# A mixture-of-experts decoder block on one core: smaller token blocks for some experts, and the last four blocks' sums kept on chip

## The chip, the cores and the metric

The kernel runs on one core of a Trainium2 chip. Its time is device time in microseconds (us) for one execution of the whole block; three timed runs of the kernel before gave a median of 1283.62 us (1282.87 to 1284.56). Beside them one execution was recorded by the hardware profiler. Times in the traces count from the start of that execution's span. TensorE is called PE and its weight loads PEld, VectorE DVE, ScalarE ACT, GpSimd POOL and SyncE SP.

## The reference

One decoder layer for 1024 tokens of width 1024, all in float32: a conditioned norm, attention and a gated branch, then a mixture of 32 experts in 4 groups of 8, and a final RMS norm. A token picks one group and two experts in it. Cut to what the change touches:

```python
g_idx = argmax(lg); top_p, top_i = top_k(softmax(le of that group), 2)
expert_id = g_idx * 8 + top_i                       # two experts of one group per token
yb = (silu(xb @ w_gate[e]) * (xb @ w_up[e])) @ w_down[e]   # 1024 -> 512 -> 1024, blocks of rows xb of expert e
x = x + g2 * segment_sum(yb * row_weight, token)
y = x * rsqrt(mean(x * x) + eps) * final_g          # final norm
```

Which tokens an expert gets is known only at run time. With these inputs the 32 experts get between 8 and 226 of the 2048 token places.

## The kernel before, in words

The first stage, up to about 682 us, ends with the router. This document is about the second stage, from there to the end: 32 units, one per expert. The first four units are expert 0 of each group, fixed when the kernel is built, so that their weights and rows can be fetched before the routing is sorted. The other 28 are taken from a list that the kernel sorts at run time: groups by their largest expert, and experts within a group by their count. `PLAN` gives the rows that a place in that list may hold, `TURNS` the order in which the places are taken. A unit whose count exceeds its rows would go through a loop at the very end, which with these inputs is not entered.

A unit needs gate, up and down weights, 2 MiB each. They come through `ring2`, a ring of seven 2 MiB buffers of the pool `big`: SP issues load k (line 1343) when the buffer of load k-7 has been read. The order is gate of unit u, down of unit u-1, up of unit u. The work itself is a list of jobs (`jobs2`), four to a load. Functions hooked onto a job are put into the program behind it: the gather of rows by POOL (`gather`, line 1364), the transposes on PE (`x_t`, `a_t`), `silu` and `mul`, and `y_out`, which scales the result on DVE (lines 1506, 1510) and adds its rows to the residual array `x1d` in DRAM by an indirect DMA on POOL (line 1493).

Blocks come in two sizes. In a **128-row block** each weight piece of 128x1024 is split into a high and a low part, by a cast on ACT (line 443) and a subtraction on DVE (line 444), two jobs ahead of its use; the parts lie in the pool `h2p` with four buffers each; PE makes three passes (`mm3`, lines 132 to 134). In a **64-row block** the raw weights are read by PE directly (`PSH`, line 1432): two instructions, one for each half of the 128 columns of the array, so that the two halves of the output columns are computed side by side. So the buffers of a 128-row block come free when DVE has split them, those of a 64-row block when PE has read them.

While the first units run, `table` (hooked on jobs 7 to 14) makes the row lists of all other blocks from one-hot products on DVE, POOL and PE, once for whole blocks and once for halves.

At the end `f_load` (line 1725), hooked onto the down jobs of the third last unit but queued on SP behind all loads of the ring, issues eight loads of 512 KiB that bring `x1d` back, and then the last unit's down weights in four parts. The results of the last two blocks (`ends`, both of 64 rows) are not added in DRAM: their rows of `x1d` are gathered, added and normed apart. `final` (lines 1781 to 1817) squares the eight token tiles on ACT (line 1736), scales them on DVE (line 1746), and stores everything by POOL's indirect DMAs (line 1764): the tiles without the rows of the last two blocks (`rows_o` sends those out of bounds), and these rows by themselves.

## Time and profile before

| | |
|---|---|
| timed runs | 1283.62 us median of 3 (1282.87 to 1284.56) |
| the profiled execution's own time | 1281.95 us |
| its span | 1280.3 us |
| expert stage | about 682 us to the end of the span |
| TensorE busy | 1189.3 us, 93% of the span |
| VectorE, ScalarE, GpSimd busy | 820.0, 595.2 and 236.3 us |
| moved by DMA | 334.25 MB, mean 261 GB/s over the span |

The share of a whole span hides that the first stage is limited by arithmetic and moves little, while the second moves 192 MiB of expert weights. So the second is read by stretches: for each the busy time of the engines, the share of the DMA engines, and who waited for whom. A DMA share of 1 means that all sixteen engines had packets all the time; the rows about SP's queue tell which buffer a load waited for before it could even be issued.

### The profile page before, as it was taken

The page shows a single profiled execution, that of the slowest core. Times are in us where ns is not written, and L with a number is a line of the kernel's source. Part 1 is how long each engine was busy: PE and PEld are TensorE (multiplying, and loading weights), DVE is VectorE, ACT ScalarE, POOL GpSimd, SP SyncE. Part 2 cuts the span into 40 slices and gives each one's busy share as a digit, 9 for nine tenths or more (in the row PEclk, how much of TensorE's full clock was granted, in tenths as well). Part 3 has the DMA queues.
Part 4 walks back from the last instruction along what each step waited for, and adds up shares of the span by engine and source line. Part 5 has one row for each costly group of instructions (what it writes and reads, how often), then busy time and mean ns, then how long its engine had stood idle before and what let it go on. Part 6 is the DMA issues. An engine that isn't in the chain of part 4 may idle for free. (4 is left out here: it accounts for less than half of the span.)

```text
span 1280.3 us, 17327 instructions
## 1 busy us (share of the span) xinstructions
PE 1189.3 (93%) x6243; PEld 911.5 (71%) x6244; DVE 820.0 (64%) x1699; ACT 595.2 (46%) x1005; POOL 236.3 (18%) x262
## 2 busy tenths in 40 slices
PE   6999999999989999899997999999999999899881
PEld 3788887788879888688875786676665655776540
DVE  7668885568667888344598896675434612984406
ACT  4459743236535774233345585563314512773321
POOL 3510010011140001010233322212112121111114
PEclk8899999999989999899996999999999999999996
DMA  9634446566443435534766699999999999999975
GB/s 321 216 108 124 132 135 203 174 212 230 131 169 118 127 127 183 179 99 147 288 245 233 215 366 405 400 406 399 376 333 405 383 336 407 409 411 390 412 274 218
DMA packets 106885, 334.25 MB, mean 261 GB/s; under 512 B 8883, under 2 KB 52611, under 8 KB 82344
## 3 DMA queue, kind: packets, MB, share of 16 engines
q1 hardware_dynamic: 91286, 292.46, 60.3%
q0 software_dynamic: 15408, 40.59, 10.7%
q8 instruction: 50, 0.82, 0.3%
q14 instruction: 43, 0.35, 0.1%
q10 hardware_dynamic: 98, 0.03, 0.0%
HBM read 315.98 MB, written 27.54 MB: 268 GB/s over the span
## 5 line engine op out<-in xcount | busy, mean ns | idle before, releaser
L444 DVE TENSOR_TENSOR lo<-big,hi 128x1024 fp32r<-128x1024 f32 x192 | 227.7, 1223 | 44.8 <-ACT hi L443 44.3
L132 PE MATMUL ps<-big,hi 128*128 128x512 f32 x544 | 220.3, 405 | 7.8 <-ACT hi L443 7.8
L443 ACT CAST hi<-big 128x1024 fp32r<-128x1024 f32 x192 | 196.4, 1050 | 60.9 <-PE ps L134 58.3
L133 PE MATMUL ps<-big,hi 128*128 128x512 f32 x544 | 217.1, 399 | 3.3 <-DVE big L444 3.3
L134 PE MATMUL ps<-big,lo 128*128 128x512 f32 x544 | 216.3, 398 | 0.0
L443 ACT CAST hi<-st 128x512 fp32r<-128x512 f32 x192 | 116.1, 619 | 204.2 <-PE ps L133 120.1
L444 DVE TENSOR_TENSOR lo<-st,hi 128x512 fp32r<-128x512 f32 x192 | 135.5, 717 | 105.5 <-ACT hi L443 104.8
L1432 PE MATMUL ps<-big,xTh 128*64 128x256 f32 x1088 | 128.8, 383 | 0.0
L132 PEld LDWEIGHTS ps<-big,hi 128*128 128x128 f32 x544 | 105.3, 193 | 31.4 <-ACT hi L443 9.3
L133 PEld LDWEIGHTS ps<-big,hi 128*128 128x128 f32 x544 | 105.2, 193 | 29.4 <-DVE big L444 4.8
L134 PEld LDWEIGHTS ps<-big,lo 128*128 128x128 f32 x544 | 104.8, 193 | 23.1 <-DVE lo L444 1.1
L133 PE MATMUL ps<-lo,xTh 128*128 128x512 f32 x272 | 110.5, 406 | 8.4 <-DVE lo L444 8.3
L132 PE MATMUL ps<-hi,xTh 128*128 128x512 f32 x272 | 112.2, 414 | 6.2 <-ACT hi L443 6.2
L134 PE MATMUL ps<-hi,xTl 128*128 128x512 f32 x272 | 108.8, 400 | 0.3 <-DVE xTl L444 0.3
L1432 PEld LDWEIGHTS ps<-big,xTh 128*64 128x64 f32 x1088 | 74.5, 137 | 43.1 <-issue 4.6
L132 PE MATMUL ps<-hi,big 128*128 128x256 f32 (+1 forms) x256 | 88.4, 346 | 0.0
L133 PE MATMUL ps<-lo,big 128*128 128x256 f32 (+1 forms) x256 | 86.8, 339 | 0.7 <-DVE lo L444 0.7
L134 PE MATMUL ps<-hi,big 128*128 128x256 f32 (+1 forms) x256 | 86.5, 338 | 0.0
L1432 PE MATMUL ps<-big,aTh 128*64 128x512 f32 x272 | 64.7, 614 | 8.7 <-DMA big<-in_w_down_dram 8.7
L133 PEld LDWEIGHTS ps<-lo,xTh 128*128 128x128 f32 x272 | 52.0, 191 | 23.2 <-DVE lo L444 12.9
L132 PEld LDWEIGHTS ps<-hi,xTh 128*128 128x128 f32 x272 | 51.8, 191 | 23.3 <-ACT hi L443 9.2
L1469 DVE TENSOR_TENSOR sl<-sl,ps 128x512 f32<-128x512 f32 (+1 forms) x34 | 18.8, 552 | 70.0 <-PE ps L1432 48.1
(365 smaller groups left out, 1942.6 us busy)
## 6 DMA issues: line engine op xcount, KB each, us to landing
big<-in_w_gate_dram SPq DMA_DIRECT2D x32, 2048.0 KB
big<-in_w_up_dram SPq DMA_DIRECT2D x32, 2048.0 KB
big<-in_w_down_dram SPq DMA_DIRECT2D x30, 2048.0 KB
st<-in_w_in_dram SPq DMA_DIRECT2D x26, 1024.0 KB
st<-in_w_ada_dram SPq DMA_DIRECT2D x16, 1024.0 KB
st<-in_w_o_dram SPq DMA_DIRECT2D x10, 1024.0 KB
big<-in_x_dram SPq DMA_DIRECT2D x16, 512.0 KB
bias<-biasd POOLq DMA_DIRECT2D x16, 512.0 KB, 4.6
```

The source lines that it names most:

```text
L132: PE.matmul(ps, lh, rh, start=start, stop=False)
L133: PE.matmul(ps, lh, rl, start=False, stop=False)
L134: PE.matmul(ps, ll, rh, start=False, stop=stop)
L443: ACT.copy(hi, src)
L444: return DVE.tensor_tensor(lo, src, f(hi), op=OP.subtract)
L1432: PE.matmul(ps[64 * c:64 * c + 64], xt[:, j, 64 * h:64 * h + 64], w[:, n * c:n * c + n], start=start, stop=stop)
L1469: DVE.tensor_tensor(s, s, PS.pop((i, "u"))[:, 0:s.shape[1]], op=OP.mult)
```

## The change

In short: three of the four first experts, which were 128-row blocks, become 64-row blocks (`FIRST`, `FIRST_ROWS`: one group's first expert, that of group 1, stays whole and goes first). In `PLAN` the 13 whole blocks stay, of its 17 halves six become 32-row blocks, for which `side` uses four column groups of 32 columns. So the stage has 14 whole, 14 half and 6 quarter blocks where it had 17 whole and 17 half. The array `x1d` is called `zd`. `TURNS` of one group is changed so that the last four blocks have 64, 32, 32 and 32 rows; these four are now `ends`: their rows of `zd` are gathered in the second last unit (`z_get`), and their results stay on chip. The last four units thus add nothing to `zd`, and `f_load` is hooked onto the down jobs of the second last unit; its place in SP's queue stays. The output is now stored in two steps: the eight tiles whole, by SP's queue, and then the rows of the last four blocks over them, by POOL. Tables are made once, for 128 rows, and the lists for halves and quarters are folded from them (`rows_table`); `visits` takes the second part of a split expert into account. `tab_tok` makes six products per tile where it made two. `h2p` has three buffers, not four.

```diff
+        ((128, 64), (128,), (128,), (64,), (64,), (32,), (32,)),
+        ((128,), (128,), (64,), (64,), (64,), (64,), (32,)),
+        ((128,), (128,), (64,), (64,), (32,), (32,), (32,)))
+FIRST = (1, 0, 2, 3)
+FIRST_ROWS = (128, 64, 64, 64)
-TURNS = ((5, 1, 0, 2, 6, 3, 4), (1, 3, 4, 0, 5, 2, 6), (2, 0, 3, 4, 1, 5, 6), (0, 2, 3, 4, 1, 5, 6))
+TURNS = ((5, 1, 0, 2, 4, 3, 6), (1, 3, 4, 0, 5, 2, 6), (2, 0, 3, 4, 1, 5, 6), (0, 2, 3, 4, 1, 5, 6))
...
         for k in range(2):
-            PE.matmul(ps, A[:, k], C[:, k], start=(t == 0 and k == 0), stop=(t == 7 and k == 1))
+            at = dict(start=(t == 0 and k == 0), stop=(t == 7 and k == 1))
+            PE.matmul(ps[0:64, 0:4], A[:, k, 0:64], V[:, k, 0], **at)
+            PE.matmul(ps[64:128, 0:4], A[:, k, 64:128], V[:, k, 1], start=at["start"], stop=False)
+            PE.matmul(ps[64:128, 0:4], A[:, k, 0:64], V[:, k, 2], start=False, stop=at["stop"])
...
-    ends = flat[-2:]
+    ends = flat[-4:]
...
+    def z_get(i):
+        with tc.issue_after(R["gather"].ins), tc.issue_after(adds[-1][1].ins):
+            g_ = fetch(Z[i], zd, IDX[i][1], parts(i))
...
-    def PSH(ps, xt, h, j, w, n, start, stop):
-
-        for c in range(2):
-            PE.matmul(ps[64 * c:64 * c + 64], xt[:, j, 64 * h:64 * h + 64], w[:, n * c:n * c + n], start=start, stop=stop)
+    def side(c, ps, xt, i, w, inner, start, stop):
+
+        n, q = rows_of[c], parts(c)
+        m = w.shape[1] // q
+        for e in range(q):
+            cols_w = w[:, m * e:m * e + m]
+            if inner and q == 4:
+
+                cols_w = w.rearrange("k (h p j) -> k h j p", h=2, j=2)[:, e // 2, e % 2]
+            PE.matmul(ps[n * e:n * e + n, 0:m], xt[:, n * i:n * i + n], cols_w, start=start, stop=stop)
...
-            if u < NE - 1:
-                jobs2.hook(jd, lambda pv=pv: each(y_out, pv))
-            if u == NE - 2:
-                jobs2.hook(jd, lambda: f_load())
+            jobs2.hook(jd, lambda pv=pv: each(y_out, pv))
...
+        if u == NE - 2:
+            jobs2.hook(jg[1], lambda: each(z_get, ends))
+    f_at = jd
...
-    h2p = p2.enter_context(tc.tile_pool(name="p2hl", bufs=4, reuse_waits="tile"))
+    h2p = p2.enter_context(tc.tile_pool(name="p2hl", bufs=3, reuse_waits="tile"))
...
+    def f_put(t):
+        xt = F["x"][t // 4][:, t % 4]
+        DVE.scalar_tensor_tensor(xt, xt, fs[:, t:t + 1], FG, op0=OP.mult, op1=OP.mult)
+        SP.dma_start(out[t * P:t * P + P, :], xt)
+
+    def l_sq(j):
+        z, y = (t[ends[j]][:, 0:D // parts(ends[j])] for t in (Z, YL))
+        DVE.tensor_tensor(z, z, y, op=OP.add)
+        ACT.activation(y, z, AF.Square, accum_out=fs[:, 8 + j:9 + j])
...
+            mul(ends[3])
+            a_t(ends[3])
+            for j in range(3):
+                l_sq(j)
+            for t in range(4):
+                f_sq(t)
+            rsqrt(wk, fs[:, 0:4], 4, 1.0 / D)
+            for t in range(4):
+                f_sq(4 + t)
+                f_put(t)
+            rsqrt(wk, fs[:, 4:8], 4, 1.0 / D)
+            l_norm(0, 3)
+            for k in range(4):
+                d_mm(ends[3:], k, F["w"])
+            f_put(4)
+            f_put(5)
+            y_out(ends[3])
+            l_sq(3)
+            f_put(6)
+            f_put(7)
+            l_norm(3, 4)
+            for j in range(4):
+                l_put(j)
+    jobs2.hook(f_at, f_load)
```

`l_norm` folds the sums of squares of a split row by products on PE, takes the root, and scales each column part by itself; `l_put` stores one of the four blocks' rows.

TensorE at the head of the stage, where the first units meet. Before, behind the down projection of the first unit (`xg` are gathered rows that are transposed, `hi` and `lo` the parts of split weights, `tV` a table):

```order
L1392 MATMUL ps_7731<-ident,xg_7449 128x128 x4
L1392 MATMUL ps_7738<-ident,xg_7449 128x128
L1678 MATMUL ps_7508<-tV_7693,tA_7689 128x68 x2
L1687 MATMUL ps_7509<-tV_7693,tA_7702 128x68 x2
L1392 MATMUL ps_7738<-ident,xg_7449 128x128 x3
L132 MATMUL ps_7753<-hi_7679,xTh_7433 128x512
L133 MATMUL ps_7753<-lo_7680,xTh_7433 128x512
L134 MATMUL ps_7753<-hi_7679,xTl_7434 128x512
```

The same place now (`big` are raw weights, `ps_7787` the second unit's up projection, `ps_7816` the third unit's gate):

```order
L1790 MATMUL ps_7748<-y_7737,fold 128x68
L1439 MATMUL ps_7775<-ident,xg_7557 128x128 x4
L1495 MATMUL ps_7787<-big_7017,xTh_7550 64x256 x16
L1495 MATMUL ps_7816<-big_7419,xTh_7774 64x256 x4
L1543 MATMUL ps_7821<-ident,sl_7679 128x128 x2
L1495 MATMUL ps_7816<-big_7419,xTh_7774 64x256 x12
L1495 MATMUL ps_7842<-big_7421,aTh_7824 64x512 x8
```

The three-pass products of the second to fourth unit are gone, and with them their splits on ACT and DVE; one table product per tile is left, and two fold products follow the last one.

GpSimd at the end of the program. Before (`y` are results added to the residual array, `big` its eight tiles, `xg` the rows of the last two blocks):

```order
L1493 DMA x1d<-y_11686,tok_h 2048x512
L1364 DMA xg_11792<-x1d,late_i 128x512
L1364 DMA xg_11796<-x1d,late_i 128x512
L1764 DMA out_dram<-big_11691,rows_o 1024x1024 x4
L1764 DMA out_dram<-big_11692,rows_o 1024x1024 x3
L1764 DMA out_dram<-xg_11792,tok_h 2048x512
L1764 DMA out_dram<-xg_11796,tok_h 2048x512
L1764 DMA out_dram<-big_11692,rows_o 1024x1024
```

And now, from the last add on (`z` are the gathered rows of the last four blocks, `big_11833` their results):

```order
L1412 DMA zd<-y_11456,rows_i 4096x256
L1407 DMA z_7406<-zd,rows_i 128x512
L1407 DMA z_7409<-zd,rows_i 128x256
L1407 DMA z_7412<-zd,rows_i 128x256
L1407 DMA z_7415<-zd,rows_i 128x256
L1412 DMA out_dram<-big_11833,rows_i 2048x512
L1412 DMA out_dram<-big_11833,rows_i 4096x256 x3
```

The stores of the eight tiles have left GpSimd for SyncE's queue; four stores are left, all behind the last tile.

VectorE at the end. Before, from the fifth tile on:

```order
L1746 SCALAR_TENSOR_TENSOR big_11692<-big_11692,fs,hi_11599 128x1024 x2
L1506 SCALAR_TENSOR_TENSOR y_11882<-ps_11863,w_h,g2h 128x512
L1792 TENSOR_TENSOR xg_11796<-xg_11796,y_11882 128x512
L1746 SCALAR_TENSOR_TENSOR big_11692<-big_11692,fs,hi_11599 128x1024
L1742 COPY fs<-ps_11891 128x2
```

And now (behind three roots, the last of them that of the first three of the four blocks):

```order
L1869 SCALAR_TENSOR_TENSOR big_11833<-z_7406,fs,fgr 64x512 x2
L1869 SCALAR_TENSOR_TENSOR big_11833<-z_7409,fs,fgr 32x256 x4
L1869 SCALAR_TENSOR_TENSOR big_11833<-z_7412,fs,fgr 32x256 x4
L1847 SCALAR_TENSOR_TENSOR big_11786<-big_11786,fs,fgr 128x1024 x2
L1569 SCALAR_TENSOR_TENSOR y_7416<-ps_11929,w_sb,g2r 32x256 x4
L1852 TENSOR_TENSOR z_7415<-z_7415,y_7416 128x256
L1847 SCALAR_TENSOR_TENSOR big_11786<-big_11786,fs,fgr 128x1024 x2
L1863 COPY fs<-ps_11960 128x1
```

A block of 32 rows takes four small products where one stood, and ten of them, two of 64 rows and eight of 32, lie between the tiles' products.

## Rows read from the trace of the kernel before

**Rows 1.** The view by stretches of time over the whole expert stage. Columns: stretch in us from the span's start, its length, busy us of PE, PEld, DVE, ACT and POOL (instructions in brackets), the granted clock of TensorE (1 is full speed), the busy share of the sixteen DMA engines, GB/s.

```profile
680.00:740.00 60.00, 52.18 (x249) 41.54 (x250) 52.76 (x119) 34.89 (x41) 19.96 (x25) 0.89 0.63 222
740.00:910.00 170.00, 165.10 (x876) 120.79 (x875) 118.47 (x131) 93.92 (x112) 38.72 (x21) 1.00 1.01 394
910.00:940.00 30.00, 30.00 (x151) 21.25 (x150) 12.59 (x13) 10.99 (x14) 3.37 (x2) 1.00 0.89 343
940.00:1020.00 80.00, 77.80 (x453) 49.91 (x451) 34.84 (x38) 28.34 (x37) 16.78 (x12) 1.00 1.01 390
1020.00:1040.00 20.00, 20.00 (x122) 11.12 (x122) 8.36 (x10) 5.26 (x8) 3.40 (x3) 1.00 0.81 290
1040.00:1220.00 180.00, 170.14 (x960) 115.33 (x958) 96.16 (x103) 78.08 (x99) 30.58 (x22) 0.99 1.02 403
1220.00:1240.00 20.00, 20.00 (x134) 10.00 (x132) 1.17 (x2) 2.90 (x6) 2.79 (x3) 1.00 0.56 194
1240.00:1252.00 12.00, 3.28 (x28) 1.89 (x24) 3.40 (x16) 8.03 (x16) 2.11 (x2) 0.77 1.02 404
1252.00:1281.00 29.00, 6.34 (x18) 2.12 (x18) 17.16 (x42) 2.00 (x6) 12.94 (x10) 0.62 0.48 189
```

**Rows 2.** What SyncE's DMA queue waited for between 740 and 1240 us: line, releaser, us in total, times, longest.

```profile
SPq L1343 <- DVE lo L444: 218.9, 40, 9.6
SPq L1343 <- PE ps L1432: 198.1, 41, 14.0
SPq L1728 <- DMA x1d<-y,tok_h: 24.7, 1, 24.7
```

**Rows 3.** The same view of TensorE, same stretch.

```profile
PE ps L132 <- ACT hi L443: 9.0, 6, 2.1
PE ps L133 <- DVE lo L444: 7.5, 11, 1.1
```

**Rows 4.** The timeline of SyncE's queue: start us, us, line, the transfer issued, count; two pieces of it, at the head and at the end of the stage. A ring load moves 2 MiB.

```profile
733.50 0.39 SPq L1343 DMA_DIRECT2D big<-in_w_gate_dram  x1
...
743.93 0.38 SPq L1343 DMA_DIRECT2D big<-in_w_up_dram  x1
...
1212.53 0.37 SPq L1343 DMA_DIRECT2D big<-in_w_up_dram  x1
1237.72 4.01 SPq L1728 DMA_DIRECT2D big<-x1d  x8
1241.97 4.23 SPq L1348 DMA_DIRECT2D big<-in_w_down_dram  x4
```

**Rows 5.** The timeline of TensorE, columns as in rows 4, with the tile shape of the array (128\*64: two column groups of 64) and the operand's shape. First a load's worth of a 64-row gate or up projection, then the first and the last of 21 consecutive matmuls of a 128-row block, then the period of one 64-row unit after another and its down projection.

```profile
970.35 3.67 PE L1432 MATMUL ps<-big,xTh 128*64 128x256 f32 x32
...
976.25 0.40 PE L132 MATMUL ps<-hi,xTh 128*128 128x512 f32 x1
...
980.92 0.40 PE L134 MATMUL ps<-hi,xTl 128*128 128x512 f32 x1
...
1048.67 4.54 PE L1432 MATMUL ps<-big,xTh 128*64 128x256 f32 x40
...
1056.22 3.60 PE L1432 MATMUL ps<-big,aTh 128*64 128x512 f32 x16
...
1060.43 1.95 PE L1432 MATMUL ps<-big,xTh 128*64 128x256 f32 x16
```

**Rows 6.** Groups of instructions between 740 and 1240 us by line and shape: count, busy us, mean ns, idle time before them and its releasers. The weight load of a 64-row block, the two steps of a 128-row block's weight split, and a 256-column product on VectorE.

```profile
L1432 PEld LDWEIGHTS ps<-big,xTh 128*64 128x64 f32 x1066 | 72.9, 137 | 42.3 <-issue 4.6 <-ACT hi L443 1.8 <-DMA big<-in_w_up_dram 0.3
...
L444 DVE TENSOR_TENSOR lo<-big,hi 128x1024 fp32r<-128x1024 f32 x168 | 198.6, 1221 | 44.7 <-ACT hi L443 44.3
...
L1469 DVE TENSOR_TENSOR sl<-sl,ps 128x256 f32<-128x256 f32 x16 | 6.7, 421 | 37.6 <-PE ps L1432 37.6
...
L443 ACT CAST hi<-big 128x1024 fp32r<-128x1024 f32 x166 | 169.4, 1051 | 44.3 <-PE ps L134 42.6 <-DMA big<-in_w_gate_dram 1.1 <-PE ps L1651 0.3
```

**Rows 7.** The DMA view of 1180 to 1240 us: mean busy share of the sixteen engines in tenths, in 40 slices of 1.5 us.

```profile
DMA  9999999999999999999999999988776645743208
```

**Rows 8.** The view of line 1343 (the ring's loads), 1180 to 1240 us: who waited for a load, in total and how often.

```profile
  PEld ps L1432: 0.3, 1
```

**Rows 9.** The timeline of the end: TensorE's last two pieces, the first of ScalarE's squares, VectorE, and GpSimd's last store.

```profile
1239.16 3.62 PE L1432 MATMUL ps<-big,xTh 128*64 128x256 f32 x32
...
1252.54 5.75 PE L1432 MATMUL ps<-big,aTh 128*64 128x512 f32 x16 [8.66 <-DMA big<-in_w_down_dram]
...
1244.24 1.06 ACT L1736 ACTIVATE fj<-big 128x1024 f32<-128x1024 f32 x1
...
1252.51 4.87 DVE L1746 SCALAR_TENSOR_TENSOR big<-big,fs,hi 128x1024 f32<-128x1024 f32 x4
1257.30 0.17 DVE L192 TENSOR_SCALAR rsq<-fs 128x4 f32<-128x4 f32 x1
...
1259.68 2.48 DVE L1746 SCALAR_TENSOR_TENSOR big<-big,fs,hi 128x1024 f32<-128x1024 f32 x2
1262.08 0.75 DVE L1506 SCALAR_TENSOR_TENSOR y<-ps,w_h,g2h 128x512 f32<-128x512 f32 x1
...
1271.71 0.97 POOL L1764 DMA_INDIRECT out_dram<-big,rows_o  x1 [0.30 <-POOLq L1827]
```

**Rows 10.** The timeline of TensorE before the first expert: the products that make the first experts' token list.

```profile
680.06 1.87 PE L944 MATMUL ps<-tC,tA 128*128 128x4 f32 x8
```

More of the change, by code (lines that the diff above doesn't have):

```diff
@@ L802, in evb @@
                 DVE.scalar_tensor_tensor(gb, gb, 1.0, banks[1][s], op0=OP.add, op1=OP.mult)
-                POOL.tensor_tensor(ga, ga, gb, op=OP.add)
+                p_ = POOL.tensor_tensor(ga, ga, gb, op=OP.add)
+                with tc.issue_after(p_.ins):
+                    for step in R["later"][:8]:
+                        step()
+                    del R["later"][:8]
                 for i, m in enumerate(M[h]):
@@ L1296, in slot @@
         return 4 + 7 * g + r
[L1297 to L1299 removed]
+    for j in range(4):
+        units.append([j])
+        group[j], rows_of[j] = j, FIRST_ROWS[j]
     for i in range(7):
@@ L1511, in y_out @@
         if i in ends:
-            R["y", i] = y
             return
-        st_ = y_add(y, idx, half)
-        if i != "x":
-            grp = group[i]
-            first = i < 4
-            for j, g, other in adds:
-                if first == (j < 4) and (g != grp or i >= NE and other is adds[-1][2]):
-                    tc.declare_no_dep(st_.ins, other.ins, reason="a token's two experts are of one group")
-            adds.append((i, grp, st_))
+        st_ = put(zd, IDX[i][1], y, parts(i), compute_op=OP.add)
@@ L1523, in each @@
+        for j, other in adds:
+            if (i < 4) == (j < 4) and (group[j] != group[i] or i >= NE and other is adds[-1][1]):
+                tc.declare_no_dep(st_.ins, other.ins, reason="a token's two experts are of one group")
+        adds.append((i, st_))
     def each(fn, cs_):
```

461 lines of the change are left out of this document (242 added, 219 removed).

## The prediction

> **What bounds the kernel now.** I read the stage by stretches first [rows 1]. From 740 to 910, 940 to 1020 and 1040 to 1220 us the DMA share is 1.01 to 1.02 while TensorE is busy 94 to 97% of the time: two limits lie almost on each other. Outside these stretches the transfers rest: share 0.63 in 680 to 740, 0.89 in 910 to 940, 0.81 in 1020 to 1040, 0.56 in 1220 to 1240. Which of the two is late is told by the waits. SP's queue waits 417 us in 81 waits for a buffer that a split or a matmul still holds [rows 2]; TensorE waits 16.5 us in all for splits [rows 3] and 0.3 us for one load, the last up weights [rows 8]. So TensorE's reading holds back the loads, and the loads, once issued, run with no reserve. A faster TensorE gains only as long as the DMA engines still have idle time. What they need is read from the ring: 81 loads are issued from 743.93 to 1212.53 [rows 4], 468.6/81 = 5.79 us each, or 17.4 us a unit.
>
> **What TensorE needs.** The 21 matmuls from 976.25 to 980.92 are 20 steps of 0.233 us; a 128-row block has 72 of them, 16.8 us, and with its transposes some 18.5 us. A 64-row unit repeats after 1060.43 - 1048.67 = 11.8 us: 3.67 us each for gate and up, 3.60 us for down, the rest transposes [rows 5]. So a whole unit is slower than its 17.4 us of transfer, a half is faster.
>
> **Quarters.** No row shows a 32-row block. It has as many instructions as a half, each with half the columns. If four groups run side by side as two do, gate and up take 3.67/2 = 1.84 us and down 1.8 us or less, with transposes about 6 us. From above: each weight load (137 ns [rows 6]) and matmul in turn; a half's 32 instructions in 3.67 us are 115 ns each with two side by side, so about as much for one alone at half the columns; 64 x (137 + 115) ns for gate and up, 16 x (137 + 225) ns for down and 1 us of transposes make some 23 us. From below, nothing less than 4 us. I take 6 us: in rows 5 and 6 a half's 32 loads alone, in turn, would be 4.4 us, more than the 3.67 us that loads and matmuls took together, so the groups do overlap. The Trainium skill ("TensorE: Matmul & The Clock Gate", Part 3, The mechanism) says that weight loads overlap running matmuls only when their row groups differ; here all groups share all rows, so by that rule the 23 us would hold. By the rows just named, the trace does not agree for two groups; for four it is open.
>
> **Sum over TensorE.** Three first units save 18.5 - 11.8 = 6.7 us each, six quarters 11.8 - 6 = 5.8 us each: 20 + 35 = 55 us. The stage's loads cannot follow by as much; what counts is how much earlier the last up weights arrive (L, about 1238.7: TensorE's wait of 0.3 us ends there, and its row of 32 matmuls begins in the piece at 1239.16 [rows 8, 9]).
>
> **Head: -11 us (-4 to -14).** The load at 733.50 waits until the second unit's up weights are read. With the second to fourth units as halves TensorE passes that place about 7 us sooner, the place of 743.93 about 10, later ones 13 and more. But from about 728 on loads are then issued faster than one per 5.79 us, and the queue becomes full; only what was idle before comes back. In 680 to 740 that is 0.37 x 60 = 22 us, of which the first half lies ahead of any buffer that could be freed sooner. Tables may hold it back (-4), a stream with no gap at all until 785 gives -14.
>
> **Dips: -5 us (0 to -8).** Idle DMA time is 0.11 x 30 = 3.3 us and 0.19 x 20 = 3.8 us, 7.1 us together, where whole units stand close and TensorE held the buffers. With the stream ahead by then, most returns; the block of four whole units keeps some.
>
> **First token list: +1.5 us (0 to +4).** The products before the first gather are 24 where 8 took 1.87 us [rows 10]; only those of the last tiles stand on the path, and halves may overlap.
>
> **Splits with three buffers: 0 (0 to +1 us a whole block).** A split takes 1.05 us of cast and then 1.22 us of subtraction [rows 6]; with three buffers it may begin when the matmuls three jobs back are done, two jobs of 6 x 0.233 = 1.4 us ahead of its own. The cover is 2.8 - 2.3 = 0.5 us; with four buffers it was 1.9. Where ACT or DVE has other work, PE waits a little more than rows 3 show. A unit may lose what the transfers leave it, so small losses cost nothing; the rival below is the large one.
>
> **Queue of the last loads: part of L.** SP waits 24.7 us for the last add before it loads the residual array [rows 2], until 1237.72. Now this add comes four units earlier, and the eight loads stand right behind the last up weights. That looks like 20 us, but is not: the DMA share falls slowly, from 9 at 1222 to 3 at 1234 and 0 at 1237 [rows 7], so the engines finish one after the other, and the slowest brings the up weights only at L. About 2 us are gained here.
>
> **Tail: from L to the end, +8 us (+3 to +12), those 2 us counted.** Before it was 1280.3 - 1238.7 = 41.6 us. Now, on DVE: squares of four tiles end at about L + 8.5 (ACT's first began at 1244.24, L + 5.5, behind the last copy, which a quarter brings sooner); root 2.4 us (1257.30 to 1259.68): 11; four tiles 4.9: 16; root: 18; for three blocks copies 0.5, root 2.4, two products of 512 columns at 0.75, eight of 256 at 0.42: 26; two tiles 2.5: 28.5; last result four at 0.42 and an add: 30.5; two tiles: 33; copy, root, four at 0.42: 37. Before, only two pieces of 512 stood between the tiles [rows 6, 9]. Then POOL's four stores, which must also wait until the tiles' stores have landed (33 and some 4 us): four at 1.3 us, the last beginning at L + 41. The end came 1280.3 - 1271.71 = 8.6 us after that start: L + 49.8, against 41.6.
>
> **Sum.** -11 - 5 + 1.5 + 8 = -6.5 us against the profiled execution's 1281.95: 1275.5. The median of the runs lies 1.7 us above that execution, so I predict 1277.
>
> **Rivals.** (a) *The stream gains more.* The head gives 14, the dips 8, the tail costs 3 to 5: about -18, 1265. For it: 55 us of TensorE time are spared, three times what I count. Against it: the tail's chain of DVE instructions is certain in order. (b) *TensorE stays the bound because splits run out of cover; slower.* With three buffers each of the 13 later whole blocks would lose time. TensorE has 55 us less work, but whole units stand in runs, where each already takes more than its transfer; once a whole block loses over about 1.5 us the gain of the stream is gone, and at 2.5 us it is 12 to 15 us later than in my sum: about 1290. For it: the cover of 0.5 us, and waits on both split steps already [rows 3]. Against: DVE has far less to do (rows 6: 1.22 us x 12 per unit no longer split). (c) *Quarters run one after the other.* At 23 us six quarters are longer than the transfers, four of them near the end: 1300. (d) *The clock falls.* When transfers are the bound TensorE rests between loads; after the rest of 1240 to 1252 its clock was 0.62 in the last stretch, partly the lower of the two levels (1.2 GHz), and 16 matmuls took 5.75 instead of 3.60 us [rows 1, 5, 9]. A half at that pace takes 19 us, more than its transfer: some 10 us late, 1286. The Trainium skill ("TensorE: Matmul & The Clock Gate", HAM oscillation) describes it: short bursts between waits for DMA each start at the lower clock. That the clock is 1.00 from 740 to 1240 shows only that it did not happen while TensorE was busy. (e) *The transfer was the bound anyway.* Share 1.01 nearly all the time: head and dips give 4 together, the tail costs 8: 1287.
>
> **How the numbers follow.** My case 0.54 (its own range 1270 to 1284); (a) 0.18, (b) 0.10, (c) 0.06, (d) 0.05, (e) 0.07. The range 1262 to 1290 leaves out (c) and the ends of (a) and (b). About 2.6 us, 0.2%, is what a measurement of this kernel can tell from no change. Of my case some 0.80 lies below 1281, 0.15 within: faster 0.43 + 0.18 = 0.61, and a little from (d) and (e): 0.64; same 0.08 + 0.06 from these two: 0.14; slower 0.22.
>
> **What would show it.** Right: the load of the fifth unit's gate at about 726; a DMA share of 1 from about 728 on without dips; TensorE waiting for loads, not SP for buffers, in the second half; quarters of 6 us; the residual loads issued within a few us of the last up weights; a longer chain on DVE behind them, ending in four stores on POOL. Wrong: waits of TensorE for `hi` or `lo` of over 20 us (b), a quarter's gate above 3 us (c), a clock below 0.9 within the stage (d), the last up weights not before 1234 (e).

## The result, and the profile after

The changed kernel took 1292.62 us (median of 16 runs, 1284.61 to 1297.75), the kernel before 1284.09 us (16 runs on the same chip). The ratio is 1.0061, its 95% interval 1.0046 to 1.0077: about 8 us slower, where 7 us faster was predicted, and outside the range. The profiled execution after had a span of 1291.2 us and took 1292.86, close to the median; that of before (1281.95) lies 2.1 us below the median of its 16 runs.

I cut both spans at two events: the load at which SP leaves the first stage (before at 665.58, after at 669.28), and the moment when the last up weights are there (L; before about 1238.7, after 1238.31, where PE's row of 64 matmuls ends a wait for them).

| piece, us | before | after | difference | predicted |
|---|---|---|---|---|
| first stage, to SP's load | 665.6 | 669.3 | +3.7 | 0 |
| from there to L | 573.1 | 569.0 | -4.1 | -14.5 (head -11, dips -5, token list +1.5) |
| from L to the end of the span | 41.6 | 52.9 | +11.3 | +8 |
| span | 1280.3 | 1291.2 | +10.9 | -6.5 |

So the stage's gain was there, but small; the first stage and the end took more than it gave. These are readings of one profile of each kernel; by how much they differ between executions is said below. In the following fences the columns are those of the groups named.

The timeline of SP after, as in [rows 4]: the head, then the end.

```profile
669.28 0.37 SPq L1382 DMA_DIRECT2D big<-in_w_gate_dram  x1
...
732.65 0.39 SPq L1382 DMA_DIRECT2D big<-in_w_gate_dram  x1
...
740.23 0.38 SPq L1382 DMA_DIRECT2D big<-in_w_up_dram  x1
...
1207.27 3.12 SPq L1382 DMA_DIRECT2D big<-in_w_up_dram  x1
1210.56 27.96 SPq L1838 DMA_DIRECT2D big<-zd  x8
1239.54 3.98 SPq L1387 DMA_DIRECT2D big<-in_w_down_dram  x4
```

The load that stood at 733.50 comes 0.9 us sooner, the next up weights at 740.23 in place of 743.93: the halves pull ahead as predicted, but from a start that is late. At the end the last up weights are asked for 5.3 us sooner (1207.27, before 1212.53) and still arrive at the same time: 31 us after their issue, where it was 26. The eight loads of the residual array stand right behind them, as predicted. The last down weights are asked for 1.2 us after L; that row serves as the mark of L below (before it stood 3.3 us after L, at 1241.97).

The stretches of [rows 1] after, the last two long ones cut at other places.

```profile
680.00:740.00 60.00, 50.68 (x274) 33.62 (x273) 38.53 (x134) 21.34 (x28) 18.91 (x29) 0.82 0.67 238
740.00:910.00 170.00, 157.66 (x858) 106.64 (x857) 92.48 (x106) 69.42 (x88) 29.38 (x21) 0.97 1.01 403
910.00:940.00 30.00, 30.00 (x150) 21.13 (x150) 13.51 (x14) 11.20 (x14) 2.64 (x2) 1.00 0.90 341
...
1020.00:1040.00 20.00, 20.00 (x134) 11.21 (x134) 8.18 (x11) 3.48 (x7) 4.14 (x3) 1.00 0.85 316
...
1140.00:1200.00 60.00, 57.45 (x436) 38.80 (x438) 29.89 (x34) 21.81 (x30) 13.24 (x10) 0.97 0.98 365
1200.00:1220.00 20.00, 15.12 (x255) 9.66 (x251) 2.21 (x4) 1.57 (x5) 3.03 (x3) 0.91 1.02 410
1220.00:1240.00 20.00, 11.05 (x206) 8.42 (x202) 4.13 (x9) 0.92 (x3) 0.00 (x0) 0.78 1.00 409
```

680 to 740 has a DMA share of 0.67, where 0.63 was; the dips at 910 and 1020 us are still there (0.90 and 0.85, before 0.89 and 0.81); and a new one stands at 1140 to 1200, 365 GB/s where [rows 1] have 403 over that part. PE is busy 30 of 30 and 20 of 20 us in the old dips: there it is still PE that holds the buffers. Over the whole of 740 to 1240 us SP's queue still waits 402 us for buffers that PE or a split holds, where it was 417 [rows 2]:

```profile
SPq L1382 <- PE ps L1495: 205.5, 47, 10.9
SPq L1382 <- DVE lo L449: 196.1, 35, 9.3
```

From 1200 us on PE rests between loads. It spares time where the transfers cannot use it.

TensorE's timeline and its waits (as in [rows 3], 740 to 1292 us) show both ends of this.

```profile
1207.78 2.06 PE L1495 MATMUL ps<-big,xTh 128*32 128x128 f32 x64
1213.39 0.66 PE L1495 MATMUL ps<-big,xTh 128*32 128x128 f32 x16 [3.56 <-DMA big<-in_w_gate_dram]
...
1238.31 3.45 PE L1495 MATMUL ps<-big,xTh 128*32 128x128 f32 x64 [3.08 <-DMA big<-in_w_up_dram]
```

```profile
PE ps L135 <- ACT hi L448: 15.1, 10, 2.1
PE ps L136 <- DVE lo L449: 12.1, 17, 1.3
...
PE ps L1495 <- DMA big<-in_w_down_dram: 8.2, 5, 5.2
...
PE ps L1495 <- DMA big<-in_w_gate_dram: 5.7, 2, 3.6
...
PE ps L1495 <- DMA big<-in_w_up_dram: 5.4, 2, 3.1
```

A quarter's up projection is 64 matmuls in 2.06 us: four groups do run side by side, though there are twice as many instructions as in a half, where the prediction said as many. PE waits 19.3 us for loads. Of these 5.6 are for the last down weights, for which it waited 8.7 before [rows 9]; for the 13.7 us of the others it had 0.3 before [rows 8]. It waits 27.2 us for splits, where it was 16.5 [rows 3].

The head differs from execution to execution, and all later readings of one profile depend on it. Until the first expert's matmuls begin TensorE works in short pieces, and it is then at the lower of its two clock levels, 1.2 GHz (granted clock 0.50). In this execution it stays there for 9.2 us, from 693.05 to 702.24, though it works without a gap. In a profile of the same program with another order of the very end (e6_tail, below) it stays there for 2.7 us, from 695.95 to 698.68. The stretches of this one, then of that one, columns as in [rows 1]:

```profile
692.00:696.00 4.00, 4.00 (x10) 1.69 (x8) 4.00 (x15) 1.38 (x3) 1.03 (x1) 0.50 0.42 145
696.00:700.00 4.00, 4.00 (x10) 3.03 (x10) 2.44 (x10) 1.63 (x2) 0.00 (x0) 0.50 0.02 6
700.00:704.00 4.00, 4.00 (x11) 2.36 (x11) 1.97 (x3) 2.08 (x3) 0.00 (x0) 0.74 0.46 96
```

```profile
695.00:699.00 4.00, 4.00 (x12) 2.15 (x11) 4.00 (x16) 1.93 (x4) 1.03 (x1) 0.68 0.35 118
699.00:703.00 4.00, 4.00 (x17) 2.66 (x15) 3.83 (x10) 2.71 (x4) 0.00 (x0) 1.00 0.01 4
```

The 6.5 us more at half the clock are 3.2 us of work done later, and the difference stays to the end: L comes 569.0 us after SP's load here and 565.7 us there. The profiles of the changed kernel's variants below fall in the same two groups, whatever was changed in them. With 2.6 to 2.8 us at the lower level (four profiles) SP asks for the last down weights 566.1 to 567.4 us after its first load, with 7.0 to 9.2 us (seven profiles) 569.7 to 571.2. Outside these two groups lie only the variant with a whole head and the one with a product left out. The kernel before has 1.9 and 4.5 us at the lower level in two profiles, and 576.4 and 576.2 us. Why the clock rises early or late is open.

The end, on VectorE and GpSimd (as in [rows 9]):

```profile
1250.90 4.87 DVE L1847 SCALAR_TENSOR_TENSOR big<-big,fs,fgr 128x1024 f32<-128x1024 f32 x4
1255.69 0.16 DVE L197 TENSOR_SCALAR rsq<-fs 128x4 f32<-128x4 f32 x1
...
1258.27 0.17 DVE L197 TENSOR_SCALAR rsq<-fs 128x3 f32<-128x3 f32 x1
...
1260.64 5.47 DVE L1869 SCALAR_TENSOR_TENSOR big<-z,fs,fgr 64x512 f32<-64x512 f32 x10
1266.15 2.48 DVE L1847 SCALAR_TENSOR_TENSOR big<-big,fs,fgr 128x1024 f32<-128x1024 f32 x2
1268.55 1.96 DVE L1569 SCALAR_TENSOR_TENSOR y<-ps,w_sb,g2r 32x256 f32<-32x256 f32 x4
...
1270.88 2.47 DVE L1847 SCALAR_TENSOR_TENSOR big<-big,fs,fgr 128x1024 f32<-128x1024 f32 x2
...
1279.56 1.01 POOL L1412 DMA_INDIRECT out_dram<-big,rows_i  x1 [72.58 <-SPq L1910]
...
1283.46 0.97 POOL L1412 DMA_INDIRECT out_dram<-big,rows_i  x1 [0.31 <-DMA out_dram<-big,rows_i]
```

One chain (the first root lies ahead of the lines shown): root, four tiles, root, root, ten products, two tiles, the last block's result, two tiles, and only then (behind the tiles' stores) POOL's four stores, the last beginning at L + 45.2 where L + 41 was worked out.

### The profile page after: what moved, and what is told of

It reads as the page before. It is cut to its first block, busy times and chain, and to the rows that moved or that the text cites. A ratio compares the mean times of both kernels' runs of the same rounds, so it can differ in the third digit from the quotient of the medians.

```text
span 1291.2 us, 18384 instructions
## 1 busy us (share of the span) xinstructions
PE 1161.4 (90%) x6766; PEld 885.5 (69%) x6766; DVE 798.8 (62%) x1728; ACT 555.5 (43%) x970; POOL 216.5 (17%) x308
## 5 line engine op out<-in xcount | busy, mean ns | idle before, releaser
L449 DVE TENSOR_TENSOR lo<-big,hi 128x1024 fp32r<-128x1024 f32 x156 | 186.2, 1222 | 65.6 <-ACT hi L448 64.9
L448 ACT CAST hi<-big 128x1024 fp32r<-128x1024 f32 x156 | 159.6, 1049 | 73.7 <-PE ps L137 73.1
L1495 PE MATMUL ps<-big,xTh 128*64 128x256 f32 (+1 forms) x1664 | 138.5, 350 | 11.2 <-DMA big<-in_w_gate_dram 5.7
L135 PEld LDWEIGHTS ps<-big,hi 128*128 128x128 f32 x544 | 105.0, 193 | 33.7 <-ACT hi L448 11.3
L1569 DVE SCALAR_TENSOR_TENSOR y<-ps,w_sb,g2r 128x512 f32<-128x512 f32 (+2 forms) x80 | 53.0, 668 | 114.5 <-PE ps L1495 88.8
L1495 PEld LDWEIGHTS ps<-big,xTh 128*64 128x64 f32 (+1 forms) x1664 | 85.7, 130 | 52.2 <-issue 22.4
L136 PE MATMUL ps<-lo,xTh 128*128 128x512 f32 x224 | 95.4, 426 | 12.2 <-DVE lo L449 12.1
L135 PE MATMUL ps<-hi,xTh 128*128 128x512 f32 x224 | 95.4, 427 | 9.5 <-ACT hi L448 9.5
L137 PE MATMUL ps<-hi,xTl 128*128 128x512 f32 x224 | 93.2, 416 | 0.0
L1407 POOL DMA_INDIRECT xg<-h2d,rows_i x30 | 34.7, 1158 | 289.1 <-PE ps L1449 164.8
L1495 PE MATMUL ps<-big,aTh 128*64 128x512 f32 (+1 forms) x416 | 65.6, 517 | 8.2 <-DMA big<-in_w_down_dram 8.2
```

The costliest lines, as they stand in the source:

```text
L135: PE.matmul(ps, lh, rh, start=start, stop=False)
L136: PE.matmul(ps, lh, rl, start=False, stop=False)
L137: PE.matmul(ps, ll, rh, start=False, stop=stop)
L448: ACT.copy(hi, src)
L449: return DVE.tensor_tensor(lo, src, f(hi), op=OP.subtract)
L1407: return POOL.indirect_dma_start(out=t[0:n, 0:D // q], out_offset=None, in_=in_parts(src, q), in_offset=bass.IndirectOffsetOnAxis(ap=idx[0 ...
```

## The experiments

All times are medians of timed runs beside the kernel before on the same chip; a ratio is to that kernel. 0.1% is 1.28 us.

### Are the splits' three buffers the cost?

Two kernels ask it from both sides: the changed kernel with four buffers (for room, the norm weights and the kept blocks' results are moved into freed split buffers; the lines for this are left out), and the kernel before with three.

```diff
-    h2p = p2.enter_context(tc.tile_pool(name="p2hl", bufs=3, reuse_waits="tile"))
+    h2p = p2.enter_context(tc.tile_pool(name="p2hl", bufs=4, reuse_waits="tile"))
```

> The changed kernel with four buffers for the split weights again; the final gain and the results kept for the last four blocks lie in freed split buffers, as there is no room otherwise. Theory S (three buffers take the cover of the splits, so TensorE is late at the head and at every 128-row block): the third up load is issued about 7 us earlier than in the changed kernel (701.4), TensorE's waits for both split steps after 740 us fall from 27 to about 16 us, the last up weights arrive 4 to 8 us earlier than 1238.2, the time is about 1285 to 1288. Rival O (the new order of the units holds the loads back): no more than 2 us, about 1291. Rival T (only the first stage and the tail lost): 1292.

> The kernel before with three buffers for the split weights and nothing else changed. Theory S: slower by 5 to 10 us (1289 to 1294), since 17 blocks of 128 rows lose about 0.4 us each and the head some more, and TensorE's waits for the split steps after 740 us rise above 25 us. Rivals O and T: within 2 us of 1284.

Measured: with four buffers 1293.02 us, ratio 1.0060 (1.0038 to 1.0083), the same as the changed kernel; TensorE's waits for `hi` and `lo` stay (15.2 and 12.6 us). Its profile does have the last up weights at 1234.0, 4.3 us sooner, as theory S said. But its clock rose early at the head, and beside e6_tail, which has three buffers and an early rise, it has 566.4 us where that has 567.0; four buffers with a late rise (b1_all_four, below) have 571.2. So the fourth buffer gives the changed kernel nothing that can be told. In the kernel before, three buffers cost 0.32% (0.16 to 0.47%), some 4 us, less than the 5 to 10 of theory S, and TensorE's waits for splits did not rise (15.7 us, before 16.5). SP's rows of that kernel:

```profile
663.84 0.37 SPq L1343 DMA_DIRECT2D big<-in_w_gate_dram  x1
...
1214.32 0.37 SPq L1343 DMA_DIRECT2D big<-in_w_up_dram  x1
```

From the first to the second are 550.5 us; in the kernel before 1212.53 - 665.58 = 547.0. So 3.5 us are lost with three buffers. In that kernel the third up weights were asked for at 693.94 us and not at 689.40, though its stage had begun sooner: it is the head, made of whole blocks, that pays most of it. With halves there, the changed kernel does not notice the fourth buffer.

### The order of the turns, and one kept block fewer

```diff
-TURNS = ((5, 1, 0, 2, 4, 3, 6), ...
+TURNS = ((5, 1, 0, 2, 6, 3, 4), ...
...
-    ends = flat[-4:]
+    ends = flat[-3:]
```

> The changed kernel with the order of units of before (the fifth-largest expert of the first group goes back from the 21st place to the 29th, as a whole block) and only the last three blocks, all of 32 rows, kept on chip. Rival O: the last up weights arrive 4 us or more earlier than 1238.2 and the time is 1286 to 1288, one block less in the tail giving 2 us of it. Theory S: the arrival moves by under 2 us, the time is 1289 to 1291 by the shorter tail alone.

Measured: 1286.85 us, ratio 1.0023 (1.0004 to 1.0041), 0.38% better than the changed kernel. From SP's load at 669.27 to that of the last down weights (1236.69) are 567.4 us, 2.9 less than the changed kernel's 570.3; from there to the end 45.7 (span 1282.4), against 51.7. The 2.9 us are not the turns': 3.2 us stand already at the fourth load behind the first, where the turns are still the same, and go with the early rise of the clock; with these turns and a late rise there are 571.2 us (b2_all_three, below). So all of the gain that can be told is the shorter end. The turns do move a dip: in 1140 to 1200 us the three kernels with the old ones move 392 to 396 GB/s, six with the changed kernel's turns 364 to 369 (382 with a whole head). Its turns have a whole block in the 21st place, where the old ones have a half. But the last up weights do not come later for it.

### The head undone

```diff
-FIRST_ROWS = (128, 64, 64, 64)
+FIRST_ROWS = (128, 128, 128, 128)
...
```

With them go 12 of the small operations that make constants for the tables.

> The changed kernel with its four first blocks at 128 rows again; the rest of the change stays. Theory H (the halves at the head only let loads be issued sooner that then queue up, and the lead is gone before the end): the last up weights land within 2 us of the changed kernel's 1238 us, counted from the same start, and the time is within 3 us of the changed kernel's. Rival (the head's lead is real and is kept): the last up weights come 5 us or more later, time 1298 or more. Second rival (the halves at the head cost time, through the idle times and half-clock stretches of TensorE that show from 810 us on): no half-clock stretch before 1040 us here, and 3 us or more faster than the changed kernel.

Measured: 1299.19 us, ratio 1.0127 (1.0108 to 1.0145). My theory H fell: the head's halves are worth 0.66%, some 8 us, and the lead is kept to the end. Its rows of SP:

```profile
669.02 0.37 SPq L1380 DMA_DIRECT2D big<-in_w_gate_dram  x1
...
1246.83 2.83 SPq L1385 DMA_DIRECT2D big<-in_w_down_dram  x3
```

577.8 us from the first row to the last, against 570.3: -7.5 us for the halves. But here the clock rose early (2.6 us at the lower level); beside e6_tail, where it did too, the halves are worth 10.8 us (10.9 to L). To L this kernel, with whole blocks at the head, takes 3.5 us longer than the one before (576.6, before 573.1), the size of what three buffers cost there. So the gain of 4.1 us comes out as 3.5 - 10.9 = -7.4 with an early rise of the clock, and 3.3 lost by the late one in the changed kernel's profile; each of these rests on one profile a side.

### TensorE made faster

One of the three products of each whole block is left out (the output is then not the reference's); loads and splits stay.

```diff
-                        mm3(PS[c, key], xh_[:, k], xl_[:, k], hi[:, q], lo[:, q], k == 0, k == 7)
+                        mm2(PS[c, key], xh_[:, k], hi[:, q], lo[:, q], k == 0, k == 7)
...
```

> The changed kernel with one of the three products of each 128-row block left out (the one with the low part of the activations); loads, splits and everything else stay. A whole block takes TensorE 11 us in place of 17, less than its transfers everywhere. Theory D (transfers bound the stage nearly all the time; TensorE holds them up only in the dips at 910 to 940, 1020 to 1040 and 1140 to 1200 us): the dips close and the last up weights land 6 to 14 us earlier, at about 1224 to 1232, no more. Rival P (TensorE's pace around the whole blocks is what bounds the stage): they land 20 us or more earlier. Rival X (the transfers alone set it): within 3 us of 1238.

Measured in one profile: the last down weights are asked for at 1232.99 us, 6.6 us sooner than in the changed kernel, with the first stage's end 0.6 us later; 563.1 us in place of 570.3. The dips close:

```profile
910.00:940.00 30.00, 30.00 (x192) 19.94 (x192) 12.37 (x16) 7.76 (x12) 5.10 (x4) 1.00 1.01 376
1020.00:1040.00 20.00, 17.85 (x203) 11.46 (x204) 9.44 (x12) 6.24 (x10) 6.77 (x5) 0.95 1.00 346
1140.00:1200.00 60.00, 52.01 (x432) 30.25 (x434) 14.02 (x19) 9.62 (x18) 12.38 (x11) 0.83 1.01 387
```

Of these 7.2 us 2.6 stand already at the fourth load behind the first, at the head, where the first whole unit is faster too and the clock rose after 4.4 us. So TensorE's pace around the later whole blocks costs 4 to 5 us in this one profile, and the rest is transfers, as theory D says, though at the lower end of its 6 to 14. This is also the price of the prediction's dips (-5), which the changed kernel did not collect.

### Small units between the whole ones

```diff
+TURNS = ((1, 0, 5, 2, 3, 4, 6), (3, 5, 1, 4, 0, 2, 6), (0, 2, 3, 1, 4, 5, 6), (2, 4, 0, 3, 5, 1, 6))
```

> The changed kernel with another table of turns: the same experts in the same blocks, but small units stand between the whole ones in place of runs of four and five whole units; the last four units stay 64, 32, 32, 32 rows. Theory D (time that TensorE spares in one place does not reach another, because the ring holds only seven loads, some two units): with the small units between whole ones the dips close, above all the one at 1140 to 1200 us, and the last up weights land 4 to 10 us earlier, time 1283 to 1289. Rival X (the transfers alone set it): the same within 2 us.

Measured: 1288.01 us, ratio 1.0032 (1.0015 to 1.0049), 0.29% better than the changed kernel, at the edge of what can be told. But its profile gives little of it to the stream: 569.7 us between the two marks. The old dips close (910 to 940 us 1.02, 1020 to 1040 0.98) and another opens at 1040 to 1140 (0.92), around the unit of 128 and 64 rows and the whole unit in front of it. Neither theory is shown.

### The quarters taken out

The kernel with the old turns and three kept blocks, with 64 rows in place of 32 in `PLAN`.

> The changed kernel with the turns of before and the last three blocks kept, and with 64 rows in the six blocks that have 32. Theory Q (quarters near the end save TensorE time that the transfers cannot use): the time within 2 us of the same kernel with quarters (1286.85), the last up weights within 2 us of its 1235.3. Rival (the quarters carry part of the gain): 3 us or more slower, the last up weights at 1238 or later. Second rival (quarters cost, through TensorE's rests and half-clock stretches): 2 us or more faster.

Measured: ratio 1.0051 (1.0031 to 1.0071) against 1.0023 of the same kernel with quarters: 0.28%, some 3.6 us, but the intervals overlap, so the rival is not shown. By the mark that theory Q named it would hold: the last up projection begins at 1235.10, where 1235.3 was said. But this kernel left the first stage 3.6 us sooner, and counted from there it does not. Two rows of PE show the difference; the first is from the kernel with halves, the second from the one with quarters (e4_order3).

```profile
1235.10 3.62 PE L1495 MATMUL ps<-big,xTh 128*64 128x256 f32 x32
```

```profile
1235.45 2.08 PE L1495 MATMUL ps<-big,xTh 128*32 128x128 f32 x64 [1.68 <-DMA big<-in_w_up_dram]
```

With halves the last up projection waits for nothing: TensorE itself is the last there, 569.4 us after SP's load (at 665.69); with quarters it waits for its weights, 566.2 us after (669.27). In both the clock rose early at the head (2.7 us). So in these two profiles quarters are worth 3 us, by taking TensorE off the end of the stream, and no more.

### The first stage

The change puts 62 small operations that make constants for the tables (48 on GpSimd, 14 on VectorE) behind GpSimd's gate sums at 190 to 301 us. Three kernels: the constants at the stage's very start; in the second half of the first stage (530 to 614 us); and the kernel before with the same operations added, to tiles that nobody reads.

```diff
-                    for step in R["later"][:8]:
+                    for step in R["later"][:8 if h else 0]:
...
```

The lines are those of the second kernel.

> The changed kernel with the constants of the tables made at the start of the first stage, not in pieces of eight behind each of GpSimd's gate sums. Theory F (those pieces make VectorE wait for GpSimd in the first stage): the load at 669.3 is issued at about 665.6 as before, everything behind it 3 to 4 us earlier, the time is about 1289. If the constants cost nothing where they stand: 1292.6, no difference.

> The changed kernel with the new constants of the tables (48 small operations on GpSimd, 14 on VectorE) behind the eight gate sums of the second half, at 530 to 614 us, in place of behind those of the first half at 190 to 301 us. Theory F (the 3.6 us by which the first stage ends later are the constants on GpSimd, whose sums others wait for in the first half; in the second half TensorE is the bound and hides them): the load that stood at 669.3 us comes at 665 to 666.5, and the time falls by 2 to 4 us to 1288.5 to 1290.5. Rival (the shift comes from elsewhere, as from where tiles lie, or the constants cost the same wherever they stand): the load at 669 or later, the time within 1 us.

> The kernel before with 62 small operations more (48 on GpSimd, 14 on VectorE, written to tiles that nobody reads), eight behind each gate sum of the first half, as the changed kernel has its constants there. Theory F (the changed kernel's first stage ends 3 to 5 us later through these operations): the load that stood at 665.6 us comes at 668 to 670 and the time is 2 to 4 us (0.2 to 0.3%) above the kernel before. Rival (they cost 1 us at most and the rest of the shift is scatter between executions or another part of the change): below 667.5 us, and the time within 0.15%.

> The kernel before, unchanged, profiled once more, to see by how much its first stage differs between executions. Theory F (its first stage ends at about 665.6 us each time): the load at 665 to 666.5 us. Rival (scatter): 667 us or later.

Measured: at the start 1290.77 us, ratio 1.0050 (1.0027 to 1.0073): nothing that can be told from the changed kernel. It has the load at 671.04. In the second half 1289.96, ratio 1.0031 (1.0014 to 1.0048), 0.3% better, at the edge of what can be told; its profile has the load at 668.52, which theory F did not expect. The kernel before with the operations added: ratio 1.0027 (1.0015 to 1.0039), 3.5 us slower. The same load in SP's timeline, first of this kernel, then of the kernel before profiled once more:

```profile
667.97 0.37 SPq L1357 DMA_DIRECT2D big<-in_w_gate_dram  x1
```

```profile
665.79 0.37 SPq L1343 DMA_DIRECT2D big<-in_w_gate_dram  x1
```

It stood at 665.58 in the first profile of before, and at 663.84 in the kernel before with three buffers, whose first stage is the same. So the constants cost 0.27% (0.15 to 0.39%), 2 to 5 us, in time, and in the trace 2.2 us or more. That they make the whole 3.7 us is not shown: eight profiles with constants where the change has them put this load at 665.69 to 671.43 us (the ends are the kernel without quarters, which has 12 constants fewer, and e6_tail), four with them in the second half at 667.19 to 670.51. Moving them away did not bring back 665.6, so either they cost as much wherever they stand or another part of the change has a share.

### The end in another order, and the mends together

```diff
-            rsqrt(wk, fs[:, 4:8], 4, 1.0 / D)
-            l_norm(0, 3)
+            l_fold(0, 3)
+            rsqrt(wk, fs[:, 4:11], 7, 1.0 / D)
...
-            f_put(4)
-            f_put(5)
+            for t in range(4, 8):
+                f_put(t)
             y_out(ends[3])
             l_sq(3)
-            f_put(6)
-            f_put(7)
-            l_norm(3, 4)
+            l_mul(0, 3)
+            l_fold(3, 4)
+            rsqrt(wk, fs[:, 11:12], 1, 1.0 / D)
+            l_mul(3, 4)
```

> The changed kernel with VectorE's work behind the last loads in another order: one root for tiles 4 to 7 and the first three kept blocks together, the four remaining tiles' products directly behind it, the kept blocks' products last. The same numbers are computed. Theory T (the end is 11 us later than before by the length of VectorE's chain behind the last transfers): one root of 2.4 us less ahead of the tiles and the tiles' stores no longer behind ten products: the end 3 to 7 us nearer to the last up weights than the changed kernel's 53 us, time 1286 to 1290. Rival (the end is set by the transfers, the last down weights at 1253.8 us and the stores behind them): no change, within 2 us.

Measured: 1285.43 us, ratio 1.0009 (0.9991 to 1.0027): 0.52%, 6.7 us better than the changed kernel from the order of one chain alone. From L (1237.17) to the end its profile has 45.8 us, the changed kernel 52.9. Its VectorE, then its GpSimd:

```profile
1254.94 0.17 DVE L197 TENSOR_SCALAR rsq<-fs 128x7 f32<-128x7 f32 x1
...
1257.36 4.87 DVE L1847 SCALAR_TENSOR_TENSOR big<-big,fs,fgr 128x1024 f32<-128x1024 f32 x4
1262.15 1.96 DVE L1569 SCALAR_TENSOR_TENSOR y<-ps,w_sb,g2r 32x256 f32<-32x256 f32 x4
...
1264.49 5.47 DVE L1870 SCALAR_TENSOR_TENSOR big<-z,fs,fgr 64x512 f32<-64x512 f32 x10
```

```profile
1266.68 1.20 POOL L1412 DMA_INDIRECT out_dram<-big,rows_i  x1 [60.84 <-DVE big L1870]
...
1274.49 0.97 POOL L1412 DMA_INDIRECT out_dram<-big,rows_i  x1 [3.28 <-DVE big L1870]
```

The tiles are done at 1262, and POOL stores a block as soon as its products are done; counted from L its first store begins 11.7 us sooner than in the changed kernel, the last 7.8. The span is 1283.0.

Then the mends together: constants in the second half, four buffers and the shorter end, with the changed kernel's turns, with the old turns and three kept blocks, and with the spread turns.

> The changed kernel with the constants in the second half, four buffers of split weights, and VectorE's end in the shorter order, all together. If the costs found add up (constants 3, end 7, buffers 0 to 4 us): 1279 to 1283, some 0.2% below the kernel before. If one of them hides another: 1284 or more.

> The same three mends with the turns of the kernel before and only the last three blocks kept on chip. If the turns' 3 us in the last up weights and the end of one block less add to the mends: 1275 to 1281. If the add in front of the residual's load (until 1225 us with these turns) is what ends last: no better than with four blocks.

> The same three mends, four blocks kept, and the turns with small units between the whole ones. If those turns' 4.6 us in the time was the stream's and not the first stage's: 1276 to 1280. If it was the first stage's (in that run's profile the load stood 2.8 us earlier): the same as with the changed kernel's turns, 1279 to 1283.

Measured beside 1284.87 us of the kernel before: 1284.61, ratio 0.9992 (0.9972 to 1.0011); 1282.75, ratio 0.9973 (0.9954 to 0.9992); 1286.84, ratio 1.0004 (0.9984 to 1.0025). Each came above the range said for costs that add up. The second is faster than both kernels, by 0.27% than the one before; the third gives no sign that the spread turns bring anything. The mends do not add up: constants 0.30, end 0.52 and turns with one block less 0.38% make 1.2%, and 0.88% were gained; the last two shorten the same chain, which may be why.

## Why the prediction was wrong

- **Dips: -5 (0 to -8).** This step failed: 0. I let "the stream ahead by then" close them. It was ahead, but not by enough: counted from SP's first load, the 20th load behind it is issued 20.8 us sooner than before, the 41st, behind the first run of whole units, only 5.6, and the shares there are 0.90 and 0.85 as before. SP still waits 402 us for buffers. I argued that the ring of seven loads keeps time spared elsewhere from these runs; spreading the units, which should have shown it, did not decide it. The size was about right: 4 to 5 us came when TensorE was made faster at the whole blocks themselves.
- **Splits with three buffers: 0.** This step failed too. I looked for waits of TensorE inside later whole blocks; the cost is at the head, 3.5 us in the trace and 4 us in time for a head of whole blocks. Rival (b) had the mechanism at the wrong place: in the changed kernel a fourth buffer brings nothing. Its sign, over 20 us of waits for `hi` and `lo`, did appear (27.2), but stays with four buffers (27.8).
- **Head: -11 (-4 to -14).** Right in kind and size for the halves alone: 7.5 us in the two profiles compared, 10.8 with the clock alike. Part of it buys back the three buffers, so that 7.4 are left, and in the profiled execution 4.1, since its clock rose late. That the clock at the head could cost 3.3 us is a term that I did not have.
- **First token list: +1.5 (0 to +4).** Within its range: the first rows are transposed 21.9 us after SP's load, before 21.4; in other profiles of the changed kernel's variants 22.2 to 24.5.
- **The first stage: not in the sum.** An omission: the constants that the new tables need stand in the diff, in a stage that I did not look at, which ends 3.7 us later. They cost 2.2 us or more of this; the rest is open.
- **Quarters, 6 us.** The number of instructions was wrong, the size about right (2.06 us for an up projection, 1.93 us for a down, at the full clock; at the lower one an up projection took up to 3.5, above the 3 of the sign of (c)). They bring 3 us in the stream, through the end of it. The rule of the Trainium skill that the prediction weighed ("TensorE: Matmul & The Clock Gate", Part 3, The mechanism: weight loads overlap running matmuls only when their row groups differ) does not describe four groups of columns: 64 weight loads of 108 ns in turn would be 6.9 us, and loads and matmuls together took 2.06.
- **Queue of the last loads.** Right: the residual loads are issued right behind the last up weights, the slowest transfers set L, and no 20 us appeared.
- **Tail: +8 (+3 to +12).** Right in mechanism, 3.3 us short: the chain came link by link as written, each a little longer, and POOL's stores began only behind the tiles' stores, at L + 41 where L + 37 was worked out.

The terms missed are 3.7 for the first stage, 5.4 for the head with its token list (-9.5 worked out, -4.1 had; 3.3 of it the clock), 5 for the dips and 3.3 for the end: 17.4 us, the distance between -6.5 and +10.9. None of the rivals was it. Rival (e) came nearest, and its sign, last up weights not before 1234, appeared (1238.3). But that the stream gained 4.1 us where it said 4 is luck, since 3.3 us of clock are in it; its end of 8 us was too short, and it had no first stage. Against (c) stand the rows of the quarters. The sign of (d) appeared (0.78 in 1220 to 1240 us), but there the transfers are the bound, and the 3.3 us that the clock cost were lost at the head, before TensorE rested between loads.

## What to carry to other kernels

Time spared on one engine need not reach the places where that engine is the bound: halves at the head helped the head, quarters the last units, and the runs of whole units between them stayed as slow as they were. That the ring of 2.3 units is the reason was argued, not shown; ask of each stretch which engine is the bound there. Compare profiles only with the clock alike at the head: one and the same program differed by 3.3 us there, as much as most of these edits were worth. Read the whole diff for small operations in stages that the change is not about: 62 of them, mostly of 0.1 to 0.2 us, on an engine that others wait for cost about 3 us. And in a chain that ends the kernel, put what has a long way after it (stores) first: one root less and another order of the same work gave 7 us of the 11 that the new end had cost.

## What the runs showed of the hardware

The clock. After idle times of 1.6 and 0.8 us in which TensorE waited for a split, it ran at the lower level for some 3 us, though it had been busy without a gap before them. The view by stretches of the changed kernel, columns as in [rows 1]:

```profile
866.00:868.00 2.00, 2.00 (x11) 0.48 (x7) 0.00 (x0) 0.00 (x0) 0.00 (x0) 1.00 1.03 387
868.00:870.30 2.30, 0.70 (x6) 0.51 (x4) 1.50 (x2) 1.56 (x3) 1.04 (x1) 1.00 1.01 424
870.30:871.70 1.40, 0.56 (x2) 0.25 (x2) 1.40 (x2) 1.40 (x2) 1.38 (x1) 1.00 0.97 410
871.70:875.10 3.40, 3.40 (x10) 2.67 (x11) 2.94 (x3) 1.51 (x2) 0.21 (x1) 0.66 1.02 425
```

In the last row the granted clock is 0.66 on average, partly 1.2 and partly 2.4 GHz, and a matmul of a whole block takes 0.43 us in place of 0.23. Before, no stretch of [rows 1] between 740 and 910 us showed this; after, 740 to 910 has 0.97. The kernel before has one too, behind waits of 1.7 and 0.8 us (0.66 in 1194 to 1199 us), which the 0.99 of [rows 1] hides; the prediction's 1.00 up to 1240 us is not exact. Such a stretch costs under 2 us (eight matmuls at 0.43); the kernel with a product left out had more of them (0.83 in 1140 to 1200 us) and its stream was the fastest of all. Dearer is the late rise at the head: 3.3 us that stay to the end.

The transfers. The DMA line of that kernel between 1195 and 1235 us, in 40 slices of 1 us, and that of the changed kernel between 1195 and 1239:

```profile
DMA  8999999999999999999999888854986449944597
```

```profile
DMA  9999999999999999999999999999999999999998
```

From 1217 on the mean share falls, to 0.4 and 0.5, while the last up weights, for which TensorE waits, come only at 1231.8. That fits engines of which some have nothing left while the slowest sets the time; the view gives their mean alone, so it is not shown. But a mean share below 1 doesn't say that a faster TensorE would bring the difference.
